# Norm weights as one row spread by TensorE, one weight block's low part on VectorE, and a tile's transposes moved inside another tile's matmuls

## The chip, the cores and the metric

The kernel runs on one NeuronCore of a Trainium2 chip. Its engines work side by side, each through a queue of its own in program order: TensorE (PE; its weight loads are shown as PEld), VectorE (DVE), ScalarE (ACT), GpSimd (POOL) and SyncE (SP), whose queue issues most of the DMA transfers. The metric is the time of one execution on the device in microseconds; of several runs the median counts.

## What is computed

The reference is one step of a layer with two attention branches. What matters here is its beginning: a root-mean-square norm of each row, a per-column weight, and one large projection.

```python
def rms_norm(x, w):
    ms = jnp.mean(xf * xf, axis=-1, keepdims=True)
    return (xf * lax.rsqrt(ms + EPS)).astype(x.dtype) * w

h = rms_norm(x, norm_w) @ w_in        # x: 1024 prompt rows and 64 sample rows of 1024; w_in: 1024 x 6144
```

The columns of h are then split into queries, keys, values and gates of a stick-breaking branch and of a chunk-band branch; both attentions, their gated projections, a merge and an output projection follow. Keys and values of both branches are outputs too. All inputs and outputs are float32.

## The kernel before

The order of the work is written out by hand; nothing reorders it, so each engine executes its instructions in the order in which the program text emits them.

The 1088 rows are cut into nine tiles: eight prompt tiles of 128 rows (t = 0 to 7) and the sample tile of 64 rows (t = 8). The list TO (L207) gives the order: the sample tile first, then 0 to 7. Products are formed in fp32r, a reduced float32. To keep float32 accuracy each operand is split into a high part (a copy rounded to fp32r) and a low part (what is left), and three products are summed: high by high, low by high and high by low.

The first stage projects the columns that are wanted row by row, in eight blocks of 256 columns (NB, L208). Each block's weights are loaded in two halves of 512 rows: half 0 as `wraw`, half 1 as `wrawx`. `Weights.split` (L125) makes the high part on ScalarE (`whi`, `whix`; L115) and the low part on GpSimd, or on the engine it is given (`wlo`, `wlox`; L122).

For a tile t, these steps prepare the normed, transposed activations:
- `load_x(t)` (L212): SP issues the load of the rows into one of four buffers `xt`.
- `prep_s(t)` (L253): ScalarE squares and sums the rows (L258); GpSimd forms the reciprocal root `rs` (L248, L249).
- `prep_a(t)` (L261): VectorE multiplies the rows by `rs` and by the norm weights `nw`, in two halves of 512 columns, into one of two buffers `xn` (L266).
- `prep_b(t)` (L271): TensorE transposes `xn` in two groups of four 128 x 128 blocks (L277) into PSUM tiles `pt`; ScalarE copies the high part of each group out (L280 for the sample tile, L285 for the others) and VectorE the low part (L281, L286). The high and low parts go to `xs` for the sample tile, and to `xa`, `xm` and `xb` for the prompt tiles.

The norm weights `nw` are needed on all 128 partitions. They are loaded with one broadcast DMA that reads the row of 4 KB 128 times (L224).

Then the loop at L450 runs over blocks i and, within them, tiles (position ti in TO). For each it issues the matmuls (L464): 16 for the sample tile, 24 for a prompt tile. In the first block, the first two tiles have their matmuls sorted so that those with the high part of the weights come first. `prep_b(0)` stands after the sample tile's first four matmuls. After a tile's matmuls, while i is 0, the loop prepares later tiles: `prep_a` three positions on, `prep_b` two positions on, `load_x` seven on and `prep_s` four on (L471 to L478). `evac_nat` (L296) then takes the result out: for the sample tile its two halves are folded first (ScalarE L292, VectorE L293), and ScalarE copies to `vst` (L305), which SP stores to two places (L307, L309).

Ahead of the loop (L439 to L448) stand, in this order: the load of tile 3, `prep_s(8)`, `prep_a(8)`, `prep_s(0)`, `prep_b(8)`, `prep_a(0)`, the split of the first block's half 0 with its low part on VectorE, the split of half 1 with its low part on GpSimd, `prep_s(1)` and the load of tile 4.

The later stages (the other projections, the two attentions, the output) are not touched.

Of the kernel before, what the change touches and what calls it, by code (L numbers as in the profile page):

```python
# [8 lines left out]
F32 = mybir.dt.float32  # L9
# [7 lines left out]
D = 1024  # L17
# [4 lines left out]
NT = 9  # L22
# [10 lines left out]
def hybrid_step_kernel(ctx: ExitStack, tc: tile.TileContext, x_prompt, x_sample, c_sbk, c_sbv, c_cbk, c_cbv,  # L33
# [3 lines left out]
    V, A, G, TE, SP = nc.vector, nc.scalar, nc.gpsimd, nc.tensor, nc.sync  # L37
# [91 lines left out]
    W = Weights()  # L129
# [67 lines left out]
    psF = ctx.enter_context(tc.tile_pool(name="af", bufs=2, space=PS))  # L197
    with ExitStack() as ph:
        sx = ExitStack()
        natx = sx.enter_context(tc.tile_pool(name="natx", bufs=2))  # L200
        pn = ph.enter_context(tc.tile_pool(name="pn", bufs=2, side="right"))
        p1x = ExitStack()
        p1 = p1x.enter_context(tc.tile_pool(name="p1", bufs=2))
# [8 lines left out]
        def load_x(t):  # L212
            xt = p1.tile([128, D], F32, name="xt", bufs=4)
            SP.dma_start(xt[:rows(t)], tok(x_prompt, x_sample, t))
            xts[t] = xt
# [4 lines left out]
                   [128, 4, 256], "" if h == 0 else "x")  # L220

        load_x(8)
        nw = p1.tile([128, D], F32, name="nw", bufs=1)
        SP.dma_start(nw, norm_w[0:1, :].to_broadcast([128, D]))  # L224
        load_x(0)
        load_nat(0, 0)
        load_nat(0, 1)
# [1 line left out]
        load_x(2)  # L229
        half = pn.tile([128, 8], F32, name="half", bufs=1)  # L230
        G.memset(half, -0.5)
        wqk = pn.tile([128, 2, 64], F32, name="wqk", bufs=1)

        rbs = {}
# [18 lines left out]
        def prep_s(t):  # L253
            r = rows(t)
            sq = p1.tile([128, D], F32, name="sq", bufs=1)
            ms = p1.tile([128, 1], F32, name="ms", bufs=4)
            rst[t] = p1.tile([128, 1], F32, name="rs", bufs=4)
            A.activation(sq[:r], xts[t][:r], AF.Square, accum_out=ms[:r])  # L258
            rsqrt(rst[t][:r], ms[:r], 1.0 / D, 1)

        def prep_a(t):  # L261
            r = rows(t)
            xt = xts.pop(t)
            xn = p1.tile([128, D], F32, name="xn", bufs=2)
            for c in (slice(0, 512), slice(512, D)):
                V.scalar_tensor_tensor(xn[:r, c], xt[:r, c], rst[t][:r], nw[:r, c], op0=OP.mult, op1=OP.mult)  # L266
            xns[t] = xn
# [3 lines left out]
        def prep_b(t):  # L271
            r = rows(t)
            xn = xns.pop(t)
            for hf in range(2):
                pt = psT.tile([128, 4, 128], F32, name="pt")
                for k in range(4):
                    TE.transpose(pt[:, k, :r], xn[:r, (hf * 4 + k) * 128:(hf * 4 + k + 1) * 128], ident[:r, :r])  # L277
                if t == 8:
                    s = xs[:, hf * 4:hf * 4 + 4]
                    A.activation(s[:, :, 0:64], pt[:, :, :r], AF.Copy)  # L280
                    V.tensor_tensor(out=s[:, :, 64:128], in0=pt[:, :, :r], in1=s[:, :, 0:64].bitcast(F32),  # L281
                                    op=OP.subtract)
                    continue
                h, l = (xhl[s][hf][:, :, xc(t):xc(t) + r] for s in range(2))
                A.activation(h, pt[:, :, :r], AF.Copy)  # L285
                V.tensor_tensor(out=l, in0=pt[:, :, :r], in1=h.bitcast(F32), op=OP.subtract)  # L286
# [156 lines left out]
        prep_b(8)  # L443
        prep_a(0)
        W.split((0, 0), V)
        W.split((0, 1))
        prep_s(1)
        load_x(4)  # L448
        pend, raw1 = [], None
        for i in range(nb):  # L450
            for ti, t in enumerate(TO):
                r = rows(t)
                last = (i, ti) >= (nb - 1, NT - 3)
                ps = (psA if ti % 3 == 2 and not last else psF).tile([128, 512], F32, name="acc")[:, :256]
                ns = 2 if t == 8 else 3
                steps = [(k, n) for k in range(KT) for n in range(ns)]
                if i == 0 and ti < 2:
                    steps.sort(key=lambda e: (e[1], e[0]))
                for m, (k, n) in enumerate(steps):
                    if i == 0 and ti == 0 and m == 4:  # L460
                        prep_b(0)
                    w = W.sp[i, k // 4][n // (ns - 1)][:, k % 4]
                    x = xs[:, k] if t == 8 else xk(n % 2, k)[:, xc(t):xc(t) + r]
                    TE.matmul(ps, x, w, start=m == 0, stop=m == len(steps) - 1)  # L464
                if i == 0 and ti == 0:
                    prep_a(1)
                    prep_s(2)
                    load_x(5)
                if len(pend) >= 3 or (pend and pend[0][0] < i and ti > 3):
                    post_nat(*pend.pop(0))  # L470
                if i == 0 and ti + 2 < NT:  # L471
                    if ti + 3 < NT:
                        prep_a(TO[ti + 3])
                    prep_b(TO[ti + 2])
                    if ti + 7 < NT:
                        load_x(TO[ti + 7])
                    if ti + 4 < NT:
                        prep_s(TO[ti + 4])  # L478
                got = evac_nat(i, t, ps)
                if raw1:  # L480
                    norm_nat(*raw1)
                    pend.append(raw1[:3])
                raw1 = (i, t) + got if got else None
                if i == 0:
                    if ti == 2:
                        load_nat(1, 0)
                        load_nat(1, 1)
                        SP.dma_start(wqk[:, 0], q_norm_w[0:1, :].to_broadcast([128, 64]))
                        SP.dma_start(wqk[:, 1], k_norm_w[0:1, :].to_broadcast([128, 64]))
                if ti in (3, 6) and i > 0 or ti in (5, 6) and i == 0:  # L490
                    h = 1 if ti == 6 else 0
                    if i + 1 < nb:
                        W.split((i + 1, h))
                    if i + 2 < nb:
                        load_nat(i + 2, h)
                    elif h == 0:
                        load_raw(i + 2 - nb)
                if (i, ti) == (4, 2):
                    load_rb()
                if 0 <= 9 * i + ti - 40 < 8:  # L500
                    make_rb(9 * i + ti - 40)
                if i >= 5 and p1x is not None and not pend and not raw1 and ti >= 3:
                    p1x.close()
                    p1x = None
                    tp = sx.enter_context(tc.tile_pool(name="tp", bufs=1))
                    pad(tp, 64)
                    tms = [[tp.tile([128, 4, HF], F32R, name=f"t{n}{s}") for s in "hl"] for n in range(4)]
                    ws = sx.enter_context(tc.tile_pool(name="ws", bufs=3))
                    tq = ph.enter_context(tc.tile_pool(name="tq", bufs=3))
                    tjobs = iter(make_t(tms, tq))  # L510
                    tw = [3]
                if p1x is None:
                    tw[0] -= 1
                    if tw[0] < 0:
                        next(tjobs, None)
                if (i, ti) == (nb - 1, 5):
                    prep(0)
                if (i, ti) == (nb - 1, 6):
                    presum(1)
                if (i, ti) == (nb - 1, 7):  # L520
                    prep(1)
                if (i, ti) in ((0, 4), (2, 3)):
                    cache_load("sb" if i == 0 else "cb")
                at = {(1, 1): 0, (1, 4): 1, (1, 7): 2, (2, 1): 3}
                if (i, ti) in at:
                    cache_pair("sb", at[i, ti])
                if (i - 2, ti) in at:
                    cache_pair("cb", at[i - 2, ti])
                if (i, ti) in ((1, 1), (1, 5)):
                    for s in range(2):  # L530
                        h = ti // 4
                        for c in range(2):
                            o = 512 + c * HF
                            G.tensor_copy(xhl[s][h][:, :, o:o + 32],
                                          xs[:, 4 * h:4 * h + 4, 64 * s + 32 * c:64 * s + 32 * c + 32])
                if (i, ti) == (1, 0):
                    V.tensor_scalar(wqk[:, 0], wqk[:, 0], -0.125, None, op0=OP.mult)
# [6 lines left out]
    with ExitStack() as ph:  # L544
# [70 lines left out]
        for i in range(len(pairs)):  # L615
            bank, s1, u2, u3 = {}, {}, {}, {}
            for s in range(7):
# [9 lines left out]
                for c, (a, b) in enumerate(XC):  # L627
                    m = b - a
                    if s < 3:
                        bank[BANK[s], c] = psB.tile([128, 512], F32, name=f"b{BANK[s]}{c}")  # L630
                    ps = bank[BANK[s], c]
                    for k in range(4):
                        for e, (hl_, x) in enumerate(((0, 0), (0, 1), (1, 0))):
                            TE.matmul(ps[:, :m], w[:, hl_, k], right[s](x)[:, k, a:b], start=s < 3 and k == 0 and e == 0,  # L634
                                      stop=k == 3 and e == 2, skip_group_check=s > 2)
# [15 lines left out]
                if s == 4:  # L651
                    for c, (a, b) in enumerate(XC):
                        m = b - a
# [512 lines left out]
    acc, emitted = 0.0, 0  # L1166
    LAG = 3
    avq = []
    for i in range(len(seq) + LAG + 1):
        m = 0  # L1170
        if i < len(seq):
# [15 lines left out]
            m = int(acc) - emitted  # L1187
# [194 lines left out]
    for i in range(2):  # L1382
# [3 lines left out]
        for q, s in enumerate(OP_):  # L1386
# [14 lines left out]
            for c in range(2) if s != "b" else ():  # L1401
                if s < 3:
                    bank[OB[s], c] = (psB if s else psA).tile([128, 2, 256], F32, name=f"b{OB[s]}{c}")
                ps = bank[OB[s], c]
# [90 lines left out]
```

## Time and profile before

| | |
|---|---|
| median of 3 runs | 1000.45 us (999.62 to 1001.2) |
| span of the profiled execution | 1000.1 us |
| time of that execution outside its profile | not recorded apart from the span |
| TensorE busy | 977.8 us, 7512 matmuls |
| VectorE, ScalarE, GpSimd busy | 657.0, 472.9, 324.9 us |

The profile is one execution, taken by the hardware profiler. Each row of an order of time has a start, a duration, the engine, the source line, the operation, the tile written and the tiles read, the shape, how many instructions were merged into the row, and in brackets how long the engine had been idle before and what ended that. In the chain of waits, each row is a start, a duration and what the end of the execution hung on at that time. The rows of busy tenths cut the span into 40 slices of 25 us. Starts are in microseconds from the start of the span.

### The profile page before, as it was taken

How to read it: one execution, taken by the hardware profiler on the slowest of the kernel's cores; microseconds unless marked ns; L12 is line 12 of the kernel's file. 1: busy time of each engine (PE TensorE's matmuls, PEld its weight loads, DVE VectorE, ACT ScalarE, POOL GpSimd, SP SyncE). 2: the span in 40 equal slices, each digit the busy share in tenths (PEclk: the TensorE clock that was granted, in tenths of full speed). 3: DMA queues.
4: the chain of work that ended last, by engine and by line, in shares of the span. 5: the costliest groups of instructions: out<-in, count | busy, mean ns of one | idle time of the engine just before them, and what ended most of it. 6: DMA issues, size and time to landing. Idle time of an engine off the chain costs nothing.

```text
span 1000.1 us, 20177 instructions
## 1 busy us (share of the span) xinstructions
PE 977.8 (98%) x7512; PEld 930.8 (93%) x7512; DVE 657.0 (66%) x1233; ACT 472.9 (47%) x1075; POOL 324.9 (32%) x338
## 2 busy tenths in 40 slices
PE   5999999999999999999999999999999899999998
PEld 5999999999999999988898888898989798999998
DVE  5456674895455454099898878565766766499735
ACT  5534443444344433277676656454445434365320
POOL 3276663215445543211111101110202200386552
PEclk9999999999999999999999999999999999999999
DMA  7726577424656332786566544765656854773642
GB/s 237 224 92 221 189 249 256 150 91 150 198 155 192 102 97 85 188 228 187 146 166 159 160 114 117 206 200 152 193 150 186 253 168 147 242 224 101 196 136 89
DMA packets 180865, 169.83 MB, mean 170 GB/s; under 512 B 34912, under 2 KB 167136, under 8 KB 180640
## 3 DMA queue, kind: packets, MB, share of 16 engines
q1 hardware_dynamic: 172048, 160.23, 54.2%
q10 hardware_dynamic: 8720, 8.33, 2.6%
q8 instruction: 59, 0.97, 0.4%
q14 instruction: 38, 0.31, 0.1%
HBM read 109.78 MB, written 58.72 MB: 168 GB/s over the span
## 4 chain that ended last, share of the span: by engine, by line
PE 92%; DMA 2%; DVE 2%; ACT 1%; SPq 1%; issue 1%; POOL 1%; DVEq 0%; ACTq 0%
PE acc L464 19%; PE acc L773 18%; PE b L634 17%; PE b L1409 8%; PE o L1115 7%; PE pt L1076 6%; PE b L917 5%; PE z L1025 3%; PE z L1024 3%; PE acc L873 3%; PE pk L349 1%; DMA wrawx<-in_w_in_dram 1%; DMA gt<-d_gsb 1%; DVE be L1045 1%; PE pt L277 1%
## 5 line engine op out<-in xcount | busy, mean ns | idle before, releaser
L122 POOL TENSOR_TENSOR wlo<-wraw,whi 128x1024 fp32r<-128x1024 f32 x30 | 74.2, 2473 | 243.9 <-ACT whi L115 209.2
L773 PE MATMUL acc<-xm,whi 128*128 128x384 f32 (+1 forms) x384 | 128.5, 335 | 0.0
L1044 DVE TENSOR_TENSOR_SCAN kp<-kp,imp 64x576 f32<-64x576 f32 (+8 forms) x72 | 102.8, 1427 | 21.3 <-ACT kp L1027 21.1
L1034 ACT ACTIVATE be<-be,sm 128x640 f32<-128x640 f32 (+5 forms) x72 | 50.8, 705 | 97.1 <-DVE sm L1030 97.1
L1076 PE MATMUL pt<-ident,be 128*128 128x128 f32 (+2 forms) x608 | 90.1, 272 | 6.4 <-DVE wT L1087 3.4
L1085 ACT ACTIVATE wT<-pt 128x512 f32<-128x512 f32 (+3 forms) x130 | 63.6, 502 | 55.1 <-PE pt L1076 55.1
L1076 PEld LDWEIGHTS pt<-ident,be 128*128 128x128 f32 (+2 forms) x608 | 68.5, 140 | 18.4 <-issue 6.4
L464 PE MATMUL acc<-whi,xa 128*128 128x256 f32 x256 | 74.2, 292 | 0.0
L773 PEld LDWEIGHTS acc<-xm,whi 128*128 128x128 f32 x384 | 72.5, 189 | 1.1
L464 PE MATMUL acc<-wlox,xm 128*128 128x256 f32 x256 | 70.8, 278 | 0.0
L464 PE MATMUL acc<-whi,xm 128*128 128x256 f32 x256 | 70.8, 278 | 0.0
L464 PE MATMUL acc<-wlo,xa 128*128 128x256 f32 x256 | 70.7, 278 | 0.0
L464 PE MATMUL acc<-whix,xb 128*128 128x256 f32 x256 | 70.7, 278 | 0.0
L464 PE MATMUL acc<-whix,xm 128*128 128x256 f32 x256 | 70.6, 278 | 0.0
L1115 PE MATMUL o<-wT,vp 128*64 128x256 f32 (+1 forms) x608 | 66.7, 359 | 0.0
L1045 DVE TENSOR_TENSOR be<-be,kp 64x576 f32<-64x576 f32 (+8 forms) x72 | 60.3, 837 | 9.6
L1027 ACT ACTIVATE kp<-z 128x384 f32<-128x384 f32 (+6 forms) x112 | 54.3, 485 | 24.4 <-PE z L1025 22.9
L773 PE MATMUL acc<-xa,wlo 128*128 128x384 f32 (+1 forms) x192 | 65.4, 341 | 0.0
L773 PE MATMUL acc<-xa,whi 128*128 128x384 f32 (+1 forms) x192 | 65.3, 340 | 0.0
L773 PE MATMUL acc<-xm,wlo 128*128 128x384 f32 (+1 forms) x192 | 65.1, 339 | 0.0
L1115 PEld LDWEIGHTS o<-wT,vp 128*64 128x64 f32 x608 | 42.5, 137 | 23.7 <-issue 7.6
L773 PE MATMUL acc<-xb,whi 128*128 128x384 f32 (+1 forms) x192 | 64.0, 333 | 0.0
(298 smaller groups left out, 3017.2 us busy)
## 6 DMA issues: line engine op xcount, KB each, us to landing
wraw<-in_w_in_dram SPq DMA_DIRECT2D x35, 512.0 KB, 4.7
wrawx<-in_w_in_dram SPq DMA_DIRECT2D x13, 512.0 KB, 4.4
sq<-d_qsbT SPq DMA_DIRECT2D x32, 192.0 KB, 4.7
sq<-d_qcbT SPq DMA_DIRECT2D x32, 192.0 KB, 3.7
gt<-d_gsb SPq DMA_DIRECT2D x30, 192.0 KB, 2.7
xt<-in_x_prompt_dram SPq DMA_DIRECT2D x8, 512.0 KB, 5.1
d_kcbT<-hl SPq DMA_DIRECT2D x8, 512.0 KB, 4.5
d_qcbT<-hl SPq DMA_DIRECT2D x8, 512.0 KB, 5.6
```

The costliest lines, as they stand in the source:

```text
L122: (eng or G).tensor_tensor(out=l, in0=raw, in1=h[:].bitcast(F32), op=OP.subtract)
L464: TE.matmul(ps, x, w, start=m == 0, stop=m == len(steps) - 1)
L634: TE.matmul(ps[:, :m], w[:, hl_, k], right[s](x)[:, k, a:b], start=s < 3 and k == 0 and e == 0, stop=k == 3 and e == 2, skip_group_check=s ...
L773: TE.matmul(ps[:, :b - a], w[:, k], xk(x, k)[:, a:b], start=k == 0 and n == 0, stop=k == KT - 1 and n == 2)
L1027: A.activation(kp[:r, x:y], z[:r, :m], AF.Sigmoid, scale=-0.125)
L1034: A.activation(be[:r, :n], be[:r, :n], AF.Exp, bias=kp[:r, j:j + 1], scale=-1.0, accum_out=kp[:r, 2:3])
L1044: V.tensor_tensor_scan(kp[:r, n - 1::-1], kp[:r, n - 1::-1], im[:, ::-1], 0.0, op0=OP.mult, op1=OP.add)
L1045: V.tensor_tensor(out=be[:r, :n], in0=be[:r, :n], in1=kp[:r, 1:n + 1], op=OP.mult)
L1076: TE.transpose(pt[:kr, x, :r], be[:r, kb * 128:kb * 128 + kr], ident[:r, :r])
L1085: A.activation(w[:, sl:sl + m, q0:q0 + r], pt[:, :m, :r], AF.Copy)
L1115: TE.matmul(o[hd * 64:hd * 64 + 64, c0:c1], vv[:kr, kb, hd * 64:hd * 64 + 64], wT[b, p, j, hd, s // 4][:kr, s % 4, c0:c1], start=si == 0, ...
L1409: TE.matmul(ps[:, t], left[s](xs_, k)[:, ts_], wt_[:, k], start=s < 3 and t == k == e == 0, stop=k == 3 and e == 2, skip_group_check=s > 2 ...
```

## The change

It has three parts.

1. The norm weights are loaded as one row of 4 KB on one partition, into a buffer of the ring `xn`. GpSimd fills a row of ones. TensorE multiplies the two (one row of 128 ones by the row of weights, in two halves of 512 columns, plain float32), which writes the weights to all 128 partitions in PSUM, and VectorE copies both halves to `nw`. The copies stand ahead of the first `prep_a` in VectorE's order.
2. The low part of the first block's second half (`wlox`) is made by VectorE, not by GpSimd.
3. After the sample tile's matmuls of the first block, `prep_a(2)`, `prep_b(1)`, the load of tile 6 and `prep_s(3)` are no longer issued. They are issued inside the matmuls of tile 0, after the first eight of 24, in the order `prep_b(1)`, `prep_a(2)`, load, `prep_s(3)`. The sample tile's evacuation therefore comes ahead of them on every engine.

```diff
-        nw = p1.tile([128, D], F32, name="nw", bufs=1)
-        SP.dma_start(nw, norm_w[0:1, :].to_broadcast([128, D]))
+        nwr = p1.tile([1, D], F32, name="xn", bufs=2)
+        SP.dma_start(nwr, norm_w[0:1, :])
...
         half = pn.tile([128, 8], F32, name="half", bufs=1)
         G.memset(half, -0.5)
+        one = pn.tile([1, 128], F32, name="one", bufs=1)
+        G.memset(one, 1.0)
+        nw = p1.tile([128, D], F32, name="nw", bufs=1)
+        for c in (slice(0, 512), slice(512, D)):
+            ps = psF.tile([128, 512], F32, name="acc")
+            TE.matmul(ps, one, nwr[:, c], start=True, stop=True)
+            V.tensor_copy(nw[:, c], ps)
...
         W.split((0, 0), V)
-        W.split((0, 1))
+        W.split((0, 1), V)
...
                     if i == 0 and ti == 0 and m == 4:
                         prep_b(0)
+                    if i == 0 and ti == 1 and m == 8:
+                        prep_b(1)
+                        prep_a(2)
+                        load_x(6)
+                        prep_s(3)
...
-                if i == 0 and ti + 2 < NT:
+                if i == 0 and 0 < ti < NT - 2:
                     if ti + 3 < NT:
                         prep_a(TO[ti + 3])
                     prep_b(TO[ti + 2])
```

## The prediction

> **What bounds the kernel now.** I read the page first, then the chain of waits over the first 40 us, then the order of time engine by engine over the same stretch.
>
> ```profile
> PE 977.8 (98%) x7512; PEld 930.8 (93%) x7512; DVE 657.0 (66%) x1233; ACT 472.9 (47%) x1075; POOL 324.9 (32%) x338
> PE   5999999999999999999999999999999899999998
> ```
>
> TensorE is the bound: 977.8 of 1000.1 us. Only the first slice of 25 us has room (digit 5), and all three parts of the change lie in it. So I look for one number: when TensorE begins its unbroken row of matmuls. What comes after moves by the same amount.
>
> ```profile
> 12.05 2.97 POOL wlox L122
> ...
> 15.38 0.58 POOL rs L249
> ...
> 15.99 0.76 DVE xn L266
> ...
> 16.88 0.64 PE pt L277 x4
> ...
> 18.17 2.83 PE acc L464 x24
> ```
>
> This is the chain of waits, in order of time. The low part of the second weight block sits on GpSimd for 2.97 us; behind it in that queue waits the reciprocal root of prompt tile 1, then its normed rows, then its transposes, which stand ahead of tile 0's matmuls. From 17.5 on it is all TensorE. The change attacks just this chain; the question is which chain ends last next.
>
> TensorE's own order of time:
>
> ```profile
> 7.38 1.35 PE L277 MATMUL pt<-ident,xn 64*128 64x64 f32 x8 [7.38 <-DVE xn L266]
> 10.81 1.22 PE L464 MATMUL acc<-whi,xs 128*128 128x256 f32 x4 [2.09 <-ACT whi L115]
> 11.84 1.91 PE L277 MATMUL pt<-ident,xn 128*128 128x128 f32 x8
> ...
> 14.40 1.05 PE L464 MATMUL acc<-wlo,xs 128*128 128x256 f32 x4
> 15.25 0.94 PE L464 MATMUL acc<-wlox,xs 128*128 128x256 f32 x4
> 16.88 1.29 PE L277 MATMUL pt<-ident,xn 128*128 128x128 f32 x8 [0.69 <-DVE xn L266]
> ...
> 18.49 0.63 PE L464 MATMUL acc<-whix,xm 128*128 128x256 f32 x4
> 18.96 0.63 PE L464 MATMUL acc<-whi,xm 128*128 128x256 f32 x4
> ```
>
> Two things. TensorE runs at half its rate before about 16 us: groups of four start 0.85 us apart (14.40, 15.25), later 0.47 (18.49, 18.96), so 0.213 against 0.118 us for 256 columns. And in the slow stretch eight f32 transposes of 128 columns take about 1.7 us, 0.21 each: an f32 column costs twice a fp32r column there.
>
> VectorE's order of time:
>
> ```profile
> 6.58 1.41 DVE L266 SCALAR_TENSOR_TENSOR xn<-xt,rs,nw 64x512 f32<-64x512 f32 x2 [6.58 <-POOL rs L249]
> 9.58 0.75 DVE L281 TENSOR_TENSOR xs<-pt,xs 128x256 fp32r<-128x256 f32 x2 [1.59 <-ACT xs L280]
> 10.25 1.40 DVE L266 SCALAR_TENSOR_TENSOR xn<-xt,rs,nw 128x512 f32<-128x512 f32 x2
> 11.57 1.22 DVE L122 TENSOR_TENSOR wlo<-wraw,whi 128x1024 fp32r<-128x1024 f32 x1
> 13.92 0.69 DVE L286 TENSOR_TENSOR xm<-pt,xa 128x512 fp32r<-128x512 f32 x1 [1.13 <-ACT xa L285]
> 14.53 0.68 DVE L286 TENSOR_TENSOR xb<-pt,xm 128x512 fp32r<-128x512 f32 x1
> 15.99 1.41 DVE L266 SCALAR_TENSOR_TENSOR xn<-xt,rs,nw 128x512 f32<-128x512 f32 x2 [0.78 <-POOL rs L249]
> 17.84 1.41 DVE L266 SCALAR_TENSOR_TENSOR xn<-xt,rs,nw 128x512 f32<-128x512 f32 x2 [0.44 <-POOL rs L249]
> 19.18 0.68 DVE L286 TENSOR_TENSOR xm<-pt,xa 128x512 fp32r<-128x512 f32 x1
> ```
>
> Between 9.58 and 19.18 VectorE idles only 1.13 + 0.78 + 0.44 = 2.35 us. It is nearly as full as TensorE, and the change gives it three more operations. So its order decides as much as TensorE's.
>
> **The change, part by part.** In the list of DMA issues (last number: us to landing), of ScalarE's order of time, and of groups by shape:
>
> ```profile
> nw<-in_norm_w_dram SPq DMA_DIRECT2D x1, 512.0 KB, 5.0
> ...
> xt<-in_x_sample_dram SPq DMA_DIRECT2D x1, 256.0 KB, 3.7
> ```
> ```profile
> 0.75 0.59 SPq L214 DMA_DIRECT2D xt<-in_x_sample_dram  x1
> 1.40 0.56 SPq L224 DMA_DIRECT2D nw<-in_norm_w_dram  x1
> ```
> ```profile
> 7.99 1.06 ACT L258 ACTIVATE sq<-xt 128x1024 f32<-128x1024 f32 x1 [2.35 <-DMA xt<-in_x_prompt_dram]
> ...
> 9.16 0.66 ACT L280 ACTIVATE xs<-pt 128x256 fp32r<-128x256 f32 x2
> 9.70 1.06 ACT L115 ACTIVATE whi<-wraw 128x1024 fp32r<-128x1024 f32 x1
> ...
> 19.87 0.38 ACT L292 ACTIVATE fl<-acc 64x256 f32<-64x256 f32 x1
> 20.82 0.42 ACT L305 ACTIVATE vst<-fl 64x256 f32<-64x256 f32 x1 [0.56 <-DVE fl L293]
> ```
> ```profile
> L1087 DVE COPY wT<-pt 128x512 f32<-128x512 f32 x10 | 6.8, 683 | 1.7 <-PE pt L1076 1.7
> ```
> ```profile
> L1115 PE MATMUL o<-wT,vp 128*64 128x256 f32 x448 | 58.0, 389 | 0.0
> ```
>
> *The norm weights.* Removed: a 512 KB load that lands at 1.40 + 5.0 = 6.4, just ahead of the root that the first xn waits for (6.58). What follows in the queue lands earlier by up to 6.4 - 4.45 = 2 us; tile 0's square then no longer stands (7.99 to 9.1) ahead of the sample tile's evictions at 9.16. Added: one row of 4 KB, behind the sample tile, which lands at 0.75 + 3.7 = 4.45. The row cannot come before that, and not after 6.4, when 512 KB came: I take 4.5, as 4 KB are 1/128 of that load. Two small fills on GpSimd are over by 2 us and cost nothing.
>
> Then two f32 matmuls of 512 columns, at the slow rate. A plain f32 product with all 128 output rows has no row here; the nearest are two. The f32 transposes: 0.21 us for 128 columns at the slow rate, so 0.85 for 512. And the attention's products of f32 by f32 (last row above): 58.0 us for 448 of 256 columns, 0.13 each; two stand side by side in 64 rows each, so a pair takes 0.26 with its ends, at the full rate, and 512 columns at the slow rate at most 4 x 0.26 = 1.04. If the halves of a pair did not overlap it would be half of that. I take 0.85 each, 1.7 for the pair, and keep 1.0 and 2.1 as ends. [...]
>
> Two copies out of PSUM (0.68 each): the first hides beside the second matmul, the second is on the path. So 4.5 + 0.1 + 1.7 + 0.2 (drain) + 0.65 = 7.15: the first xn starts at 7.15 where it started at 6.58, because the spread is dearer than the end of the old load. From there: 1.41 for both halves, 0.7 for the second four transposes (1.35 in all), 0.4 and 0.4 for the last eviction and its low part: tile 0's xn starts at 10.1, against 10.25, since no square stands in the way. The high part of the first weight block follows the evictions on ScalarE (9.7 to 10.7) and TensorE's first matmul starts at 10.8, as now. The weights that land earlier gain nothing. The first part is worth nothing here.
>
> *The low part on VectorE.* GpSimd loses 2.97 us; the root of tile 1 is ready before VectorE asks. VectorE gains 1.2: tile 0's xn (10.1, spacing 1.33), first low part (11.45), second (12.65), tile 0's two low parts (13.85, 14.45), tile 1's xn from 15.1 to 16.4, against 15.99 to 17.4: 0.9 us earlier.
>
> *Tile 1's transposes after eight matmuls of tile 0.* TensorE: four matmuls at 10.8 (0.85), eight transposes (1.7), twelve matmuls at 0.213 to 15.9, eight of tile 0 at 0.118 to 16.85, tile 1's transposes (0.44 + 0.44) to 17.75, the other sixteen (1.9) to 19.6; before, tile 0's matmuls ended at about 20.8. So 1.2 us are won up to here. But tile 2's xn moved too, from ahead of tile 1's low parts to behind them and behind the sample tile's fold. ScalarE's fold copy (0.38) at 16.1, VectorE's sum at 16.5, ScalarE's copy (0.42) to 17.3; then tile 1's evictions (17.45 and 17.95), low parts (18.1 and 18.7), tile 2's xn from 19.3 to 20.7. Tile 2's transposes stand ahead of tile 1's matmuls and wait for it twice: first half at 20.05, second from 20.75 to 21.2. A new wait of some 0.8 us on TensorE, for VectorE, takes the place of the old one for GpSimd. Tile 1's matmuls start at 21.2.
>
> ```profile
> 21.63 0.36 PE L464 MATMUL acc<-whi,xa 128*128 128x256 f32 x1
> ```
>
> Before, they started at 21.63. Sum: **-0.4 us**. From there VectorE needs 2 x 0.67 + 2 x 0.6 = 2.5 us a tile against 3.7 of TensorE and does not hold it again.
>
> The same moved block issues the load of tile 6 and tile 3's square. The square follows tile 1's evictions at 18.4 and its root is there 2 us later, as tile 2's xn ends (20.7): no cost, and each us that it came later would be one on tile 3's xn, which has 2 us to spare. The load now stands on SP behind two stores of the sample tile and waits for tile 2's xn (20.7), so it is issued at about 21 and by the median of its kind lands near 26:
>
> ```profile
> xt<-in_x_prompt_dram SPq DMA_DIRECT2D x8, 512.0 KB, 5.1
> ```
> ```profile
> 29.86 1.06 ACT L258 ACTIVATE sq<-xt 128x1024 f32<-128x1024 f32 x1
> ```
>
> Its reader, tile 6's square, runs at about 29.5: 3 us of cover. If a slow load used them up, each further us would delay that tile's transposes and TensorE by a us.
>
> The profiled execution has a span of 1000.1 us; the median of the runs is 1000.45, so 0.35 lies around the span or between executions. 1000.45 - 0.4 gives **1000.1**. A measurement of this kernel can tell about 0.2%, 2.0 us: I forecast no change that can be told.
>
> **The rivals.**
> [...]
> - *The rate rises after tile 0's eight matmuls, with the cheap spread:* 0.75 us later for tile 1's transposes and all behind them, +0.35, 1000.8.
> - *The row lands late*, at 6.4 like the whole load: +1.9, of which TensorE's slack takes none: +1.5, 1002.0. Against: 4 KB.
> [...]
>
> A gain of over 2 us would need TensorE unbroken from about 15.5 at full rate; no row gives that.
>
> **How the numbers follow.** Forecast 0.45; late rate with the cheap spread 0.15; early rate 0.08; four passes 0.15, of them 0.05 with the late rate; late row 0.07; something not seen 0.10 (0.06 faster, 0.04 slower by over 2 us). The late row lies on the bound and half of it counts as slower, as do 0.03 of the four passes at the ordinary rate. Slower 0.05 + 0.03 + 0.04 + 0.04 = 0.16, faster 0.06, same 0.78. The range adds half the spread of the runs shown, 0.8 us, to the early rate and to the four passes: 998.9 to 1002.4.
>
> **What would show it.** First xn at 7.2 on VectorE behind two PSUM copies; each spread matmul at 0.85 us; no weight block on GpSimd between its first roots; tile 1's transposes at about 16.9 after eight matmuls of tile 0; a wait of TensorE for xn ahead of tile 2's transposes near 20; tile 1's matmuls from 21.2. Wrong I would be if the first xn came at 8.9, or if the wait ahead of tile 2's transposes were missing.

## The result and the profile after

The changed kernel takes 1001.64 us (median of 20 runs, 999.64 to 1003.32); the kernel before, run beside it, 999.99 us (median of 20, 998.39 to 1001.59). The ratio is 1.0015, with a 95% interval of 1.0008 to 1.0022. That is 1.65 us slower, with the whole interval above 1, where the prediction had 0.4 us faster and no change that can be told.

The page of the kernel after, busy time and TensorE's tenths:

```profile
PE 979.7 (98%) x7516; PEld 930.5 (93%) x7516; DVE 662.3 (66%) x1236; ACT 473.2 (47%) x1075; POOL 322.8 (32%) x338
...
PE   6999999999999999999999999999999899999998
```

TensorE is still the bound and only the first slice has room. One number stands out against the page of before: 7516 matmuls in place of 7512. The code adds two.

The chain of waits of the kernel after (start, duration, what the end hung on):

```profile
1.39 2.92 DMA xn<-in_norm_w_dram
...
4.45 3.76 PE acc L237 x4
...
8.85 0.75 DVE xn L273
...
11.30 1.06 ACT whi L115
...
21.34 0.75 DVE xn L273
```

GpSimd is gone from it. In its place the chain begins with the row of norm weights (landed at 1.39 + 2.92 = 4.31) and the spread, 3.76 us in four records. All that follows hangs on that: the first xn, then the weights' high part on ScalarE (held up by the evictions ahead of it), then TensorE's first matmul.

TensorE's own order of time in the kernel after:

```profile
4.45 3.75 PE L237 MATMUL acc<-xn,one 1*128 1x512 f32 x4 [4.45 <-DMA xn<-in_norm_w_dram]
...
12.41 1.23 PE L476 MATMUL acc<-whi,xs 128*128 128x256 f32 x4 [1.42 <-ACT whi L115]
...
16.84 1.05 PE L476 MATMUL acc<-wlox,xs 128*128 128x256 f32 x4
17.70 0.86 PE L476 MATMUL acc<-whi,xa 128*128 128x256 f32 x4
18.40 0.63 PE L476 MATMUL acc<-whix,xm 128*128 128x256 f32 x4
18.86 1.04 PE L284 MATMUL pt<-ident,xn 128*128 128x128 f32 x8
...
21.16 0.63 PE L476 MATMUL acc<-wlox,xm 128*128 128x256 f32 x4
22.23 1.29 PE L284 MATMUL pt<-ident,xn 128*128 128x128 f32 x8 [0.44 <-DVE xn L273]
23.27 0.36 PE L476 MATMUL acc<-whi,xa 128*128 128x256 f32 x1
```

The last line is the number that the prediction looked for: tile 1's matmuls start at 23.27, where they started at 21.63 before. That is 1.64 us later, which agrees with the 1.65 us of the runs. Two more things are to be seen. The full rate comes only at about 18 us (groups of four start 0.86 apart at 16.84, 0.70 at 17.70, then 0.47). And tile 2's transposes begin at 22.23, 0.6 us after the last matmuls of tile 0 (21.16 + 0.47), and take 1.04 us to the next matmul in place of 0.80 at 18.86: a wait of 0.6 + 0.24, some 0.85 us, for VectorE's xn.

VectorE's order of time in the kernel after:

```profile
6.53 0.69 DVE L238 COPY nw<-acc 128x512 f32<-128x512 f32 x1 [6.53 <-PE acc L237]
8.24 0.69 DVE L238 COPY nw<-acc 128x512 f32<-128x512 f32 x1 [1.01 <-PE acc L237]
8.85 1.40 DVE L273 SCALAR_TENSOR_TENSOR xn<-xt,rs,nw 64x512 f32<-64x512 f32 x2
...
11.78 1.41 DVE L273 SCALAR_TENSOR_TENSOR xn<-xt,rs,nw 128x512 f32<-128x512 f32 x2
...
16.61 1.41 DVE L273 SCALAR_TENSOR_TENSOR xn<-xt,rs,nw 128x512 f32<-128x512 f32 x2
18.35 0.42 DVE L300 TENSOR_TENSOR fl<-acc,fl 64x256 f32<-64x256 f32 x1 [0.33 <-ACT fl L299]
20.13 0.69 DVE L293 TENSOR_TENSOR xm<-pt,xa 128x512 fp32r<-128x512 f32 x1 [1.37 <-ACT xa L292]
...
21.34 1.40 DVE L273 SCALAR_TENSOR_TENSOR xn<-xt,rs,nw 128x512 f32<-128x512 f32 x2
```

The two copies start 1.71 us apart: one product of the spread takes that long, twice the 0.85 of the prediction. Tile 0's xn starts at 11.78 (10.25 before), tile 1's at 16.61 (15.99 before), although nothing on GpSimd holds it any more. Behind the sample tile's fold VectorE idles 1.37 us for tile 1's eviction, which stands behind tile 1's late transposes, and only then comes tile 2's xn.

### The profile page after: what moved, and what is told of

Read it like the earlier page. It is cut to its first block, busy times and chain, and to the rows that moved or that the text cites. A ratio compares the mean times of both kernels' runs of the same rounds, so it can differ in the third digit from the quotient of the medians.

```text
span 998.7 us, 20189 instructions
## 1 busy us (share of the span) xinstructions
PE 979.7 (98%) x7516; PEld 930.5 (93%) x7516; DVE 662.3 (66%) x1236; ACT 473.2 (47%) x1075; POOL 322.8 (32%) x338
## 4 chain that ended last, share of the span: by engine, by line
PE 93%; DVE 2%; DMA 2%; ACT 1%; issue 1%; SPq 0%; POOL 0%; DVEq 0%; ACTq 0%
PE acc L476 19%; PE acc L785 18%; PE b L646 17%; PE b L1421 8%; PE o L1127 7%; PE pt L1088 6%; PE b L929 5%; PE acc L885 4%; PE z L1037 3%; PE z L1036 3%; PE pt L284 1%; PE pk L356 1%; DVE be L1057 1%; DMA vs<-d_cbv 1%; DVE kp L1056 1%
```

## The experiments

Two theories stood against each other. The *spread theory*: the four records of the spread move VectorE's whole row, and the rest of the change would be a gain without it. The *order theory*: the loss comes from issuing tile 2's xn behind tile 1's low parts, which makes TensorE wait ahead of tile 2's transposes. Each kernel was timed beside the kernel before. The column to read beside the ratio is the start of tile 1's matmuls in the profiled execution, since the instructions behind it are the same in all of them. Their time is not: from that start to the end it is 975.0 to 978.5 us, which differs by more than the starts do, so single spans can't be compared. The last section shows part of the reason.

| kernel | first xn | tile 1's xn | tile 1's matmuls (to before) | median, us | ratio to before (95%) |
|---|---|---|---|---|---|
| before | 6.58 | 15.99 | 21.63 | 999.99 to 1000.45 | 1 |
| the whole change | 8.85 | 16.61 | 23.27 (+1.64) | 1001.64 | 1.0015 (1.0008 to 1.0022) |
| e1: part 1 alone | 8.69 | 17.36 | 23.01 (+1.38) | 1002.4 | 1.0018 (1.001 to 1.0027) |
| e2: parts 2 and 3 | 6.86 | 15.24 | 21.22 (-0.41) | 1000.3 | 0.9998 (0.9989 to 1.0008) |
| e3: whole, spread in one pass | 6.69 | 14.45 | 20.72 (-0.91) | 999.88 | 0.9994 (0.9985 to 1.0004) |
| e4: whole, order turned | 9.07 | 16.83 | 21.76 (+0.13) | 1000.83 | 1.0003 (0.9994 to 1.0012) |
| e5: parts 2 and 3, order turned | 6.67 | 14.79 | 20.59 (-1.04) | 999.88 | 0.9991 (0.998 to 1.0001) |
| e6: part 2 alone | 6.50 | 15.08 | 20.72 (-0.91) | 998.29 | 0.9984 (0.9974 to 0.9995) |
| e7: part 3 alone | 6.88 | 15.96 | 21.94 (+0.31) | 1000.45 | 0.9996 (0.9987 to 1.0005) |
| e8: one pass, order turned | 6.85 | 14.61 | 20.30 (-1.33) | 998.62 | 0.9982 (0.9973 to 0.999) |
| e9: parts 1 and 2 | 9.07 | 16.84 | 22.47 (+0.84) | 1000.68 | 1.0005 (0.9996 to 1.0014) |

In every row the shift of that start, taken as a share of 1000 us, lies within the interval of the ratio, which is some 2 us wide for most kernels.

### Part 1 alone

```diff
 # on the kernel before; the low part of half 1 stays on GpSimd, the steps of tile 2 stay where they were
-        nw = p1.tile([128, D], F32, name="nw", bufs=1)
-        SP.dma_start(nw, norm_w[0:1, :].to_broadcast([128, D]))
+        nwr = p1.tile([1, D], F32, name="xn", bufs=2)
+        SP.dma_start(nwr, norm_w[0:1, :])
...
+            TE.matmul(ps, one, nwr[:, c], start=True, stop=True)
+            V.tensor_copy(nw[:, c], ps)
```

> Part 1 alone: the kernel before with the norm weights as one row, spread by TensorE; low part on GpSimd and order as before. Theory S (the pair of f32 products costs 3.4 us, not 1.7, and holds VectorE's first xn until 8.85): the same first xn, near 8.85 instead of 6.58; tile 1's matmuls start near 22.9 instead of 21.63; +1.3 us on the time, about as much as the whole change (+1.65). Rival O (the new order, with tile 2's xn behind the sample tile's fold and tile 1's low parts, is what costs): the spread is hidden by the wait for the second block's low part on GpSimd, at most +0.3.

TensorE's order of time:

```profile
4.29 3.75 PE L237 MATMUL acc<-xn,one 1*128 1x512 f32 x4 [4.29 <-DMA xn<-in_norm_w_dram]
...
23.01 0.36 PE L471 MATMUL acc<-whi,xa 128*128 128x256 f32 x1
```

The same 3.75 us, and with nothing else changed the kernel is slower by 0.18% (0.10 to 0.27). The first xn comes 2.1 us later (8.69), tile 1's matmuls 1.38 later. So part 1 by itself carries a loss about as large as that of the whole change. The order theory can't explain it: here the order is that of before.

### Parts 2 and 3 without part 1

```diff
 # on the kernel before; the norm weights keep their 512 KB load
-        W.split((0, 1))
+        W.split((0, 1), V)
...
+                    if i == 0 and ti == 1 and m == 8:
+                        prep_b(1)
+                        prep_a(2)
+                        load_x(6)
+                        prep_s(3)
...
-                if i == 0 and ti + 2 < NT:
+                if i == 0 and 0 < ti < NT - 2:
```

> Parts 2 and 3 without part 1: broadcast load of the norm weights as before, low part on VectorE, tile 1's transposes inside tile 0's matmuls. Theory S: first xn at 6.58 again; tile 1's matmuls between 21.1 and 22.1, by when TensorE's rate rises; -0.5 to +0.5 us against before, 1.2 to 2.2 under the changed kernel. Rival O: the wait ahead of tile 2's transposes costs as it does in the changed kernel; +1 us or more against before.

TensorE's order of time:

```profile
16.43 1.03 PE L277 MATMUL pt<-ident,xn 128*128 128x128 f32 x8
...
18.72 0.63 PE L469 MATMUL acc<-wlox,xm 128*128 128x256 f32 x4
20.17 1.29 PE L277 MATMUL pt<-ident,xn 128*128 128x128 f32 x8 [0.82 <-DVE xn L266]
21.22 0.36 PE L469 MATMUL acc<-whi,xa 128*128 128x256 f32 x1
```

Tile 1's matmuls start at 21.22, where the prediction had put them for the whole change (21.2), and the time is that of before. The wait ahead of tile 2's transposes is there too (18.72 + 0.47 to 20.17, 1 us), so it belongs to part 3 and not to the spread. It eats half of what was won. The chain of waits of this kernel runs through VectorE and ScalarE as the prediction had it:

```profile
17.45 0.61 ACT xa L285
...
19.28 0.75 DVE xn L266
```

The prediction had tile 1's first eviction at 17.45 and tile 2's xn at 19.3. So the agreement is one of steps and not only of the sum, although the full rate came earlier here (14.54) than it was forecast.

### The whole change with the spread in one pass

The row and the ones are rounded to fp32r first, so the norm weights lose their low bits in this kernel.

```diff
 # on the kernel after
+        oner = pn.tile([1, 128], F32R, name="oner", bufs=1)
+        V.tensor_copy(oner, one)
+        nwh = p1.tile([1, D], F32R, name="ck", bufs=1)
+        for c in (slice(0, 512), slice(512, D)):
+            V.tensor_copy(nwh[:, c], nwr[:, c])
...
-            TE.matmul(ps, one, nwr[:, c], start=True, stop=True)
+            TE.matmul(ps, oner, nwh[:, c], start=True, stop=True)
```

> The changed kernel with the spread in one pass: the row and the ones are copied to fp32r by VectorE first, so the norm weights are rounded to fp32r (the output is computed with rounded weights). Theory S: each product 0.43 us instead of two records of 0.85; first xn near 6.9; tile 1's matmuls 1.2 to 2 us earlier than in the changed kernel (21.3 to 22.1); time -0.9 to +0.4 us against before. Rival O: the time stays at +1 us or more, since the order is the same.

TensorE's order of time:

```profile
4.65 1.22 PE L242 MATMUL acc<-ck,oner 1*128 1x512 f32 x2 [4.65 <-DVE ck L238]
...
20.72 0.36 PE L481 MATMUL acc<-whi,xa 128*128 128x256 f32 x1
```

Two records in place of four, 1.22 us in place of 3.75. Nothing else differs from the whole change but three small casts, and tile 1's matmuls start 2.55 us earlier (20.72 against 23.27). Of that, 2.17 us are there at the first projection matmul already (10.24 against 12.41); the other 0.38 belong to the full rate, which came sooner after it. The ratio goes from 1.0015 to 0.9994 (0.9985 to 1.0004). This is the run that decides: the price of the plain float32 products is what makes the change slow. The first xn (6.69) is then no earlier than with the old load (6.50 to 6.88 in the kernels without part 1), so even the cheap spread only draws level with it.

One gain does show, behind the first xn: tile 0's xn starts at 9.62 against 10.40 in e2, and tile 1's matmuls 0.50 earlier than in e2. With the smaller load tile 0's square on ScalarE runs earlier: it starts at 6.99 in the kernel after and at 7.99 in the kernel before, where the sample tile's evictions follow it at 9.16. The ratios of the two, 0.9994 and 0.9998, can't be told apart.

### The order turned

```diff
 # on the kernel after
                     if i == 0 and ti == 1 and m == 8:
-                        prep_b(1)
                         prep_a(2)
+                        prep_b(1)
```

> The changed kernel with two lines swapped: tile 2's xn ahead of tile 1's transposes, so VectorE makes it before tile 1's low parts. Theory S: the wait of TensorE ahead of tile 2's transposes (22.23 start) goes, tile 1's matmuls start near 22.5; about 0.8 us under the changed kernel, still +0.8 against before. Rival O: back at the time before or below it.

TensorE's order of time:

```profile
16.12 0.63 PE L476 MATMUL acc<-wlo,xs 128*128 128x256 f32 x4
...
20.77 1.24 PE L284 MATMUL pt<-ident,xn 128*128 128x128 f32 x8
21.76 0.36 PE L476 MATMUL acc<-whi,xa 128*128 128x256 f32 x1
```

With tile 2's xn ahead of tile 1's low parts the wait is all but gone: the transposes stand in a row with the matmuls before them, and the profile names no releaser for them; they take 0.99 us to the next matmul, 0.2 more than without a wait. The start is 1.5 us earlier than in the whole change. Some 0.65 of that is the wait. The other 0.86 is that tile 1's transposes came at 18.00 and not at 18.86, because the full rate came at about 16 us in this execution and at 18 in the other; that lies in the execution rather than in the order. The order theory is thus right on a second, smaller cost, and not on the whole: with the order mended the kernel is level with before (1.0003, 0.9994 to 1.0012) and not ahead of it, as it would be if the order were all.

### The order turned, without the spread

```diff
 # on the kernel before: parts 2 and 3, with
+                        prep_a(2)
+                        prep_b(1)
```

> Parts 2 and 3 without the spread, and tile 2's xn ahead of tile 1's transposes. Theory S (the spread's price and the order of tile 2's xn are two separate costs, 2.05 and 0.8 to 1.5 us at the start of tile 1's matmuls): no wait of TensorE ahead of tile 2's transposes, tile 1's matmuls near 20.3 to 21.2, -0.4 to -1.5 us against before. Rival (a start earlier than before is taken back elsewhere, by a wait later on): tile 1's matmuls earlier, the time as before.

TensorE's order of time:

```profile
19.32 0.64 PE L469 MATMUL acc<-wlox,xm 128*128 128x256 f32 x4
19.80 1.03 PE L277 MATMUL pt<-ident,xn 128*128 128x128 f32 x8
20.59 0.36 PE L469 MATMUL acc<-whi,xa 128*128 128x256 f32 x1
```

No wait here either (0.48 us after the start of the last group), and the start is 0.63 us before that of e2, although the full rate came 2 us later (16.57 against 14.54). The ratio of 0.9991 reaches from 0.998 to 1.0001: a gain that this measurement doesn't quite tell.

### Part 2 alone

```diff
 # on the kernel before
-        W.split((0, 1))
+        W.split((0, 1), V)
```

> Part 2 alone: the kernel before with the second block's low part on VectorE. Theory S: tile 1's xn from about 15.2 instead of 15.99, its transposes as soon as the sample tile's matmuls are done, tile 1's matmuls at about 20.9; -0.7 us against before, unless TensorE's rate rises after 16.5. Rival: VectorE's 1.2 us more take all of it, 0.0.

The chain of waits and TensorE's order of time:

```profile
11.53 1.22 DVE wlo L122
...
12.74 1.13 DVE wlox L122
...
15.08 0.75 DVE xn L266
```
```profile
14.15 0.62 PE L464 MATMUL acc<-wlo,xs 128*128 128x256 f32 x4
...
15.97 1.29 PE L277 MATMUL pt<-ident,xn 128*128 128x128 f32 x8 [0.75 <-DVE xn L266]
...
20.72 0.36 PE L464 MATMUL acc<-whi,xa 128*128 128x256 f32 x1
```

This is the whole gain of the change as it was made: both low parts run on VectorE one after the other, tile 1's xn starts at 15.08 and its matmuls at 20.72, each 0.91 us earlier than before. The kernel is 0.16% faster than before (0.05 to 0.26), the lowest median of those that compute in full precision. The size should be taken from the 0.91 us rather than from the median, for a reason given in the last section.

### Part 3 alone

```diff
 # on the kernel before: the steps of tile 2 moved into tile 0's matmuls as in the change,
 # norm weights and low parts as before
```

> Part 3 alone: tile 1's transposes, tile 2's xn, load and square inside tile 0's matmuls; low part on GpSimd, broadcast load. Theory S: the old wait for GpSimd is covered by eight matmuls, the new wait ahead of tile 2's transposes takes its place; tile 1's matmuls at 21.8 to 22.2, +0.2 to +0.5 us. Rival: the cover is a gain of 0.7 us by itself.

TensorE's order of time:

```profile
16.11 0.63 PE L469 MATMUL acc<-whix,xm 128*128 128x256 f32 x4
16.86 1.29 PE L277 MATMUL pt<-ident,xn 128*128 128x128 f32 x8
...
19.40 0.63 PE L469 MATMUL acc<-wlox,xm 128*128 128x256 f32 x4
20.89 1.29 PE L277 MATMUL pt<-ident,xn 128*128 128x128 f32 x8 [0.87 <-DVE xn L266]
21.94 0.36 PE L469 MATMUL acc<-whi,xa 128*128 128x256 f32 x1
```

The wait ahead of tile 1's transposes is filled by eight matmuls, but for some 0.3 us (16.11 + 0.47 to 16.86), and a wait of 1 us ahead of tile 2's (19.87 to 20.89) takes its place. The start moves by +0.31, the time not at all (0.9987 to 1.0005).

### One pass and the order turned

```diff
 # on the kernel after: the edits of e3 and of e4 together, norm weights rounded as in e3
```

> The changed kernel with the one-pass spread (norm weights rounded to fp32r, the output is computed with them) and with tile 2's xn ahead of tile 1's transposes. Theory S: both costs gone; first xn at 6.7, tile 1's matmuls at 19.3 to 20.7, 0.9 to 2 us faster than before. Rival: as with the run without the spread, no more than -0.5.

TensorE's order of time:

```profile
19.51 1.04 PE L289 MATMUL pt<-ident,xn 128*128 128x128 f32 x8
20.30 0.36 PE L481 MATMUL acc<-whi,xa 128*128 128x256 f32 x1
```

Tile 1's matmuls start at 20.30 with no wait ahead of tile 2's transposes, the earliest of all, and the ratio is 0.9982 (0.9973 to 0.999). Both costs of the change are gone here. The time is level with that of part 2 alone (0.9984), which needs no rounding.

### Parts 1 and 2 without the move

```diff
 # on the kernel after
-                    if i == 0 and ti == 1 and m == 8:
-                        prep_b(1)
-                        prep_a(2)
-                        load_x(6)
-                        prep_s(3)
...
-                if i == 0 and 0 < ti < NT - 2:
+                if i == 0 and ti + 2 < NT:
```

> The first two parts of the change without the third: the row spread by four f32 passes, the second low part on VectorE, and tile 1's transposes left ahead of tile 0's matmuls. If the spread's price is all of the loss and the move costs nothing beside it, tile 1's matmuls start at about 23.2 us as with the whole change, and the ratio to the kernel before is about 1.0015. If the move has a price of its own (tile 2's normed rows come too late for TensorE), VectorE's row stays as it was with the whole change (first xn 8.9, tile 1's xn 16.6), tile 1's transposes start at 17.5, tile 0's 24 matmuls at 18.5, there is no wait ahead of tile 2's transposes at 21.4, and tile 1's matmuls start at about 22.2: a ratio of about 1.0006.

TensorE's order of time:

```profile
21.68 1.04 PE L284 MATMUL pt<-ident,xn 128*128 128x128 f32 x8
22.47 0.36 PE L471 MATMUL acc<-whi,xa 128*128 128x256 f32 x1
```

The start is 22.47 and the ratio 1.0005 (0.9996 to 1.0014), between the two expected numbers and nearer to that of a move with a price. Now the loss can be told apart by starts: part 2 takes 21.63 to 20.72 (-0.91), the spread beside it 20.72 to 22.47 (+1.75), the move on top 22.47 to 23.27 (+0.80).

Not all of the 0.80 is the move's own. Take, from the table, the time from the start of tile 1's xn to tile 1's matmuls. In the four kernels with neither the move nor the turned order (before, e1, e6, e9) it is 5.63 to 5.65 us. In e2 and e7, which have the move, it is 5.98, so the move costs some 0.35 there. In e3 it is 6.27 and in the whole change 6.66, and in these two TensorE's own row sets the start of tile 1's transposes: tile 1's xn was done 0.46 and 0.84 us before it (15.86 to 16.32, 18.02 to 18.86), and groups of four began to follow at 0.47 us only 5.1 and 6.0 us after the first projection matmul, against 3.6 and 4.4 in e2 and e7. So some 0.7 us of the whole change's start (6.66 against 5.98) is a full rate that came late. It came late in e1 too (a group at 16.68 still takes 1.05 us), and cost nothing, since tile 1's transposes waited for VectorE there. The move takes that cover away.

The ratios of e9 and of the whole change have intervals that overlap (up to 1.0014, and from 1.0008 on), so the price of the move rests on the starts of single executions; that the spread is dear rests on the runs as well.

## Why the prediction was wrong

By its own steps:

- *The row lands at 4.5.* Right within 0.2: 4.31, and the first product starts at 4.45. That it can't come before 4.45 was wrong, without weight in the sum.
- *Two f32 matmuls at 0.85 each, 1.7 for the pair.* **This is the step that failed.** The pair took 3.75 us, 1.87 each, twice the price and far over the upper end of 2.1 that the prediction kept. Nearly all else that went wrong follows from it. The nearest row, the attention's products, was misread: the prediction took its 448 records for 448 products. The group of that line with both its shapes together, among the costliest groups of the page of before, shows what they are:

```profile
L1115 PE MATMUL o<-wT,vp 128*64 128x256 f32 (+1 forms) x608 | 66.7, 359 | 0.0
```

The loops at that line issue 20 steps in one branch and 18 in the other, for 2 heads and 4 pairs of heads: 38 x 2 x 4 = 304 products with `vp`. The profile lists 608, so each plain f32 product is two records, as the spread's two products are four. (The transposes of f32, also the prediction's measure, are one record each: eight for eight.) Read so, 58.0 us are 224 products of 256 columns, 0.26 each; with two side by side a pair takes 0.52 at the full rate, and 512 columns at half the rate at most 4 x 0.52 = 2.07, an estimate from that row. The upper end for the two products would have been 4.1 us, and the measured 3.75 lies below it.

The traces of the kernel after give the price beside fp32r. Four fp32r matmuls of 256 columns start 0.85 us apart at the slow rate (15.99 to 16.84), so 512 columns take 0.43, and the two copies behind the plain products stand 1.71 us apart, four times that; the start of the first product and the end of the last make it 3.75 for the pair. The chances and the range count in two more cases: four passes for a product, at 0.15 for the slow end, and an early rate, at 0.08 for the fast end. No row of before shows either term; the kernel after shows two records a product and 3.75 us for the pair, and groups of four at 0.47 us apart only from 18.40 on.

The other steps:

- *First xn at 7.15.* 8.85. The prediction's own sign of error, 8.9, appeared.
- *Tile 0's xn 2.95 us behind the first xn, since no square stands in the way.* Right: 2.93 (8.85 to 11.78).
- *The low part on VectorE wins 0.9 us; tile 1's xn at 15.1.* Right: 15.08 and 0.91 in e6.
- *The weights that land earlier gain nothing.* Right: in the kernel after, the high part of the first weights starts at 11.30, as soon as ScalarE has done the evictions ahead of it, so the wait is not for the load.
- *Tile 1's transposes at 16.85, tile 0 done at 19.6.* 18.86, and 21.63: 2 us late, of which 1.6 are the spread (TensorE's first matmul at 12.41 in place of 10.8) and the rest the full rate that came at 18. Without the spread (e2) they came at 16.43.
- *A new wait of some 0.8 us ahead of tile 2's transposes.* Right in kind, place and size: 0.85. It takes the place of the old one, as was said, and it costs more than the old one did: tile 1's matmuls stand some 0.35 us further behind tile 1's xn in e2 and e7 than without the move, and 1.0 further in the whole change with its late full rate.
- *Tile 1's matmuls at 21.2, -0.4.* Right, by the steps on ScalarE and VectorE, for the change without the spread (e2: 21.22, -0.41), wrong for the whole (23.27, +1.64).
- *0.35 us around the span.* Wrong, without weight in the sum: the profiled execution of the kernel after took 1000.91 us with a span of 998.7, so about 2.2 us lie around it. In the later runs of the kernel before it is 1.8 to 2.0; by that its profiled execution took some 1002.0 us, at the upper end of its runs.

## What to carry to other kernels

Before a duration is taken from a row, count its records against the instructions that the code issues: here a plain f32 product is two records, and a product priced by one of them comes out at half. A spread over partitions by TensorE was no cheaper here than a broadcast load that lands in time: rounded to one pass the first normed rows came no earlier with it, and in plain f32, at the start of a kernel, where groups of four fp32r matmuls started 0.85 us apart and later 0.47, it cost 1.87 us per 512 columns on the path to everything. Price each part of a bundle alone: one line here was worth 0.91 us, and the spread took back 1.75 and the move 0.35, or more where the full rate came late.

## What the runs showed of the hardware

Behind the same idle time TensorE's granted clock was 0.50 in one execution and 1.00 in another. The kernel before, in TensorE's order of time and by windows (the last three numbers are the granted clock, the share of DMA and GB/s):

```profile
575.38 1.70 PE L1076 MATMUL pt<-ident,be 128*128 128x128 f32 x8 [2.40 <-DVE wT L1087]
```
```profile
576.00:578.00 2.00, 2.00 (x10) 1.74 (x8) 1.73 (x4) 1.44 (x4) 0.10 (x1) 0.50 0.00 0
```

The kernel after has the same wait at the same place:

```profile
576.34 1.09 PE L1088 MATMUL pt<-ident,be 128*128 128x128 f32 x8 [2.40 <-DVE wT L1099]
```
```profile
576.00:578.00 2.00, 1.66 (x14) 1.48 (x16) 1.87 (x3) 0.97 (x2) 0.00 (x0) 1.00 0.24 75
```

The eight transposes take 1.09 us where they took 1.70, at a clock of 1.00. So a wait of 2.40 us was followed by half the clock once and by the full clock once; no run here shows what decides between the two.

The clock bears on the times in this document. Of the 35 runs of the kernel before beside e5 to e8, the 12 with a mean granted clock of 1.000 have a median of 999.24 us, the 19 at 0.998 one of 1000.72. For e6 it is 998.02 (6 of 11 runs) and 999.94 (4): 1.2 and 0.8 us less than before, class by class, which agrees with 0.91, while the plain medians are 2.1 apart, since more of its runs kept the clock. The classes are small, and e1 shows no such difference (1001.94 in 2 runs at 1.000, 1001.93 in 7 at 0.998). It is also part of why the span of the profiled execution is shorter after (998.7) than before (1000.1) though its first stage is longer: the halved stretch (some 3.4 us, from between 575.6 and 576.0, where the window's clock is 0.64, to between 579.0 and 579.2, where it is 0.69, with 0.50 in between) accounts, as an estimate of half its length, for some 1.7 us of the 3.0 by which the two differ behind the start of tile 1's matmuls (1000.1 - 21.63 against 998.7 - 23.27); for the other 1.3 no cause is shown.

The end of the slow stretch at the start differs between executions too: groups of four begin to follow at 0.47 us at 14.15 in e6, at 16.12 in e4 and at 18.40 in the kernel after, 3.4, 3.5 and 6.0 us after TensorE's first projection matmul. The edits don't explain it: up to there e4 and the kernel after give TensorE the same instructions. Nor does the granted clock: it reads 1.00 in the kernel before from 10.00 to 16.00, where groups start 0.85 us apart. No run shows what ends that stretch.
